# Entry of a second feed-forward on one core: where the token sums stand, and which engine shifts, scales and splits the late token tiles

## The chip, the cores and the metric

One NeuronCore of a Trainium2 chip runs the whole program. The metric is device time in microseconds of one execution; lower is better. TensorE (PE) multiplies, VectorE (DVE), ScalarE (ACT) and GpSimd (POOL) do the rest, and SyncE (SP) issues most transfers. Each engine works through its own instructions in order and waits on semaphores for the others.

## The reference

One layer of an encoder: a feed-forward, a mixer with two kinds of attention, a second feed-forward, each behind an RMS norm that is shifted and scaled. There are 512 tokens of 1024 values, in float32. What matters here is the step from the mixer's output to the second feed-forward:

```python
x = x + g2[:, None, :] * (merged @ w_out[l])
h = modulate(rmsnorm(x, ffn2_norm[l]), sh3, sc3)        # h * (1 + scale) + shift
x = x + FFN_RES_WEIGHT * g3[:, None, :] * swiglu(h, ffn2_w_in[l], ffn2_w_out[l])

def swiglu(h, w_in, w_out):
    g, u = jnp.split(h @ w_in, 2, axis=-1)               # 2 x 2816 columns
    return (jax.nn.silu(g) * u) @ w_out
```

## The kernel before

Tokens are worked on in four tiles of 128, called tile 0 to tile 3. For a precise product every matrix is split in a high part (a cast to a shorter format, on ScalarE, `split`, L202) and a low part (source minus high part, L204 on VectorE, or L208 on GpSimd), and each product is three matmuls: high by high, high by low, low by high (L223 to L225).

The mixer ends in `down`. For each token tile its last matmuls are followed on VectorE by the product with the gate (L706) and the addition to `x` (L707), on ScalarE by the sum of squares (L233), on VectorE by L240 and on GpSimd by `rstd` (L230). `norm_token` multiplies the tile by its `rstd` (L247). `turn_token`, which is held back in a list until `flush` is called, transposes the tile on TensorE (L261) in two groups of four 128x128 blocks. It shifts and scales each block on its way out of PSUM (the first of each group on VectorE, L266, three on ScalarE, L268), and splits each group into `h_hi` (ScalarE) and `h_lo` (VectorE). In the traces tiles 0 and 1 carry the name `xn` here (`xn_2_7108`, `xn_2_7141` where numbers are kept), tiles 2 and 3 `sc` (`sc4_7189`, `sc4_7243`).

The second feed-forward begins with four plain jobs in `up_plain`: job 0 and 1 are the gate and up columns of the first 128 hidden units, job 2 and 3 those of the next. A job's weights are loaded into a buffer `raw` (four of them, in turn), cast to `wh`, subtracted to `wl`. The first three jobs come in two halves: TensorE turns tile 2, does the first half of job 0 (tokens of tiles 0 and 1), the first half of job 1, turns tile 3, does the first half of job 2; then the second halves (tiles 2 and 3) of jobs 0, 1 and 2; then job 3 whole.

Behind these `up_fast` does the other hidden units with seven products in place of eight, which need sums of token blocks. `mix_tokens(0)` forms them for tiles 0 and 1, `mix_tokens(1)` for tiles 2 and 3: four additions or subtractions on VectorE (L288 to L291) and four splits (`sum_h`, `sum_l`). The fast products also need sums of weights (`w_sums`, L616 to L620, VectorE). The products read, in turn, plain tokens, then the sums `out[0]`, `out[1]`, `out[3]`, `out[2]`.

TensorE's order is the order in which the code is written. For the other engines a scheduler sets the order when the program is built.

Of the kernel before, what the change touches and what calls it, by code (L numbers as in the profile page):

```python
# [10 lines left out]
F32 = mybir.dt.float32  # L11
# [3 lines left out]
ALU = mybir.AluOpType  # L15
# [6 lines left out]
NT = S // P  # L22
# [17 lines left out]
TURN_DVE = 1  # L40
LAG_DOWN, LAG_OUT = 2, 0
EARLY_UP, FLUSH_UP = 3, (0, 2)
# [114 lines left out]
class Block:  # L157
# [85 lines left out]
    def norm_token(self, t, which, xn):  # L243
        nc = self.nc
        if which == 2 and t < 2:
            xn = self.slot([P, D], F32, "xn_2")
        nc.vector.tensor_scalar(xn, self.x[:, t], self.rstd[:, t:t + 1], None, op0=ALU.mult)  # L247
        self.pending.append(lambda: self.turn_token(t, which, xn))

    def flush(self):  # L250
# [3 lines left out]
    def turn_token(self, t, which, xn):  # L254
        nc = self.nc
        h32 = xn.rearrange("p (k c) -> p k c", k=KT)
        ts = slice(t * P, (t + 1) * P)
        for g in range(2):
            pt = self.bank("t")
            for j in range(4):  # L260
                nc.tensor.transpose(pt[:, j * P:(j + 1) * P], xn[:, (4 * g + j) * P:(4 * g + j + 1) * P], self.ident)  # L261
            for j in range(4):
                k = 4 * g + j
                sc, sh = self.scale[which][:, k:k + 1], self.shift[which][:, k:k + 1]
                if j < TURN_DVE:
                    nc.vector.tensor_scalar(h32[:, k], pt[:, j * P:(j + 1) * P], sc, sh, op0=ALU.mult, op1=ALU.add)  # L266
                else:
                    nc.scalar.activation(h32[:, k], pt[:, j * P:(j + 1) * P], AF.Identity, scale=sc, bias=sh)  # L268
            ks = slice(4 * g, 4 * g + 4)
            self.split(h32[:, ks], self.hH[:, ks, ts], self.hL[:, ks, ts])  # L270
        if which == 2:
            self.mixed.append(h32)
# [5 lines left out]
    def mix_tokens(self, j):  # L278
        ha, hb = self.mixed[2 * j:2 * j + 2]
        if not j:  # L280
            self.sum_tiles()
        a11, a12, a21, a22 = (h[:, ks] for h in (ha, hb) for ks in (slice(0, 4), slice(4, 8)))
        cs = slice(j * P, (j + 1) * P)
        self.token_sums(a11, a12, a21, a22, [[z[:, :, cs] for z in pair] for pair in self.sums])

    def token_sums(self, a11, a12, a21, a22, out):
        tt = self.nc.vector.tensor_tensor
        tt(a22, a21, a22, op=ALU.add)  # L288
        tt(a21, a21, a11, op=ALU.subtract)
        tt(a11, a22, a11, op=ALU.subtract)  # L290
        tt(a12, a12, a11, op=ALU.subtract)  # L291
        for (hi, lo), part in zip(out, (a22, a11, a21, a12)):
            self.split(part, hi, lo)

    def sum_tiles(self):
        self.sums = [[self.slot([P, KT // 2, S // 2], F32R, "sum_" + p) for p in "hl"] for _ in range(4)]
# [22 lines left out]
    def ada_columns(self, vec):  # L319
        io, nc = self.io, self.nc  # L320
        layer, kind = divmod(vec, 3)
        res = self.ring.tile([P, KT], F32, tag="adac", name="adac", bufs=2) if kind else self.shift[layer]
        for m in range(KT):
            self.ada_dot(self.ada_load(io["w_ada"][vec, m]), vec, m, res[:, m:m + 1])
            yield m == KT - 1
        if kind:
            col = (COL_FFN1, COL_MIX, COL_FFN2)[layer]
            nc.vector.scalar_tensor_tensor(
                self.scale[layer], res, 1.0, self.cols[:, col:col + KT], op0=ALU.add, op1=ALU.mult)
        yield True  # L330
# [323 lines left out]
    def act_parts(self, u):  # L654
# [14 lines left out]
        return [[z[:, j] for z in pair] for j in range(2)]  # L669

    def down(self, parts, nk, w2, layer, tail, after, lag=0, store=None, side=None):
        nc = self.nc
        nu = nk // 2
# [410 lines left out]
    def layer(self, banks):  # L1084
        nc, io = self.nc, self.io
        self.acts, self.act_pairs, self.act_seen = [], {}, []
        for f in range(F0):
            self.swiglu(f, banks[2 * f], banks[2 * f + 1])
        self.rope_angles()
        self.up_plain(io["w1a"], range(F0, F0 + F1), {0: self.mix_all})  # L1090
        gen = self.vectors((2,))
        self.up_fast(io["w1a"], range(F0 + F1, NF), WEIGHTS_A, lambda n: self.advance(gen, n > 4))
        self.x = self.fix.tile([P, NT, D], F32, tag="x16", name="x_again")
        for t in range(NT):
            nc.scalar.dma_start(self.x[:, t], io["x"][t * P:(t + 1) * P])
        late = self.vectors((4, 3, 7, 6))
        self.ada_slots = True

        def vector_steps(hf, u):
            if u > 1 if hf < 1 else u < 9:  # L1100
                for _ in range(2):
                    self.advance(late, 1)
        self.down(self.act_parts, NF, io["w2a"], 0, 3, lambda t, xn: self.norm_token(t, 1, xn), LAG_DOWN, side=vector_steps)
        self.ada_slots = False
        self.mix(lambda t, xn: self.norm_token(t, 2, xn))

        def finish(t, o32):
            z = self.slot([P, D], F32, "out")
            nc.gpsimd.tensor_tensor(z[:, :512], self.x[:, t, :512], fin[:, :512], op=ALU.mult)
            nc.vector.tensor_tensor(z[:, 512:], self.x[:, t, 512:], fin[:, 512:], op=ALU.mult)  # L1110
            nc.scalar.mul(z[:, :512], z[:, :512], self.rstd[:, t:t + 1])
            nc.sync.dma_start(io["out"][t * P:(t + 1) * P, :512], z[:, :512])
            nc.vector.tensor_scalar(z[:, 512:], z[:, 512:], self.rstd[:, t:t + 1], None, op0=ALU.mult)
            nc.scalar.dma_start(io["out"][t * P:(t + 1) * P, 512:], z[:, 512:])
        gen = self.vectors((8,))
        self.acts, self.act_pairs, self.act_seen = [], {}, []
        for t in range(NT):
            nc.scalar.dma_start(self.x_home[t], self.x[:, t])
        mixes = {EARLY_UP + j - 1: lambda j=j: self.mix_tokens(j) for j in range(2)}
        self.up_plain(io["w1b"], range(F2), mixes, EARLY_UP, FLUSH_UP)  # L1120
        self.up_fast(io["w1b"], range(F2, NF), WEIGHTS_B)
        fin = self.gate_row("final_gain")
        nc.scalar.dma_start(fin, io["final"].to_broadcast([P, D]))
        self.x = self.fix.tile([P, NT, D], F32, tag="x16", name="x_last")
        for t in range(NT):
            nc.scalar.dma_start(self.x[:, t], self.x_home[t])
        self.ada_bank = "mm"

        def side(hf, u):
            if not hf:  # L1130
                self.advance(gen, 1 if u < 9 else 99)
        self.down(self.act_parts, NF, io["w2b"], 2, 3, finish, side=side)
# [79 lines left out]
```

## Time and profile before

| | |
|---|---|
| runs (3) | median 1093.59 us, 1091.13 to 1093.73 |
| the profiled execution | 1090.79 us, of which the span of the profile is 1088.9 |
| PE busy | 1061.0 us, 97% of the span |
| DVE busy | 770.5 us, 71% |
| ACT busy | 569.2 us, 52% |
| POOL busy | 155.9 us, 14% |
| the chain that ended last | PE 88%, DVE 5%, ACT 3%, DMA 2% |

Busy shares are averages over a program of many stages. The stage of this change lies between 731 us, where the mixer's last matmuls end, and about 766 us, in the second of the fast hidden units; it has to be read by itself. A row of the timeline gives the start, the duration, the engine, the line, the operation with result and sources, and in brackets the idle time of the engine before it with what ended it. A duration holds the instruction's fixed part too, so the next instruction of an engine often starts before the row's end.

### The profile page before, as it was taken

The numbers are of one execution on the slowest core, as the hardware profiler recorded it, in microseconds if no ns is written. First come the engines' busy times: TensorE is split into PE (matmuls) and PEld (weight loads), VectorE is DVE, ScalarE is ACT, GpSimd is POOL, SyncE is SP. The second block draws the span as 40 slices with busy tenths as digits, with TensorE's granted clock in tenths as the row PEclk, the third lists the DMA queues.
The fourth block names the chain that finished last, engine by engine and source line by source line (L and its number), as shares of the span: only waits on it lengthen the run. The fifth ranks groups of instructions, "written<-read, shape, count | busy, mean of one in ns | idle before, by whom it ended". The sixth has DMA issues, their size and how long they took to land.

```text
span 1088.9 us, 16923 instructions
## 1 busy us (share of the span) xinstructions
PE 1061.0 (97%) x6496; PEld 939.4 (86%) x6496; DVE 770.5 (71%) x1277; ACT 569.2 (52%) x1066; POOL 155.9 (14%) x222
## 2 busy tenths in 40 slices
PE   4999999999999999999999999999999999999997
PEld 3789999998888898988888887888999999988885
DVE  5898898878984766666668643569887887883524
ACT  5546555564322676767667524356655655661312
POOL 1000000000000011334544477100000000000200
PEclk9999999999999999999999999999999999999999
DMA  9633454439974611122222164623333333374312
GB/s 361 256 100 106 147 159 137 132 97 350 346 259 137 235 62 39 40 78 78 80 95 78 61 206 128 245 100 109 102 98 116 116 98 98 120 252 127 103 59 78
DMA packets 43575, 152.04 MB, mean 140 GB/s; under 512 B 5219, under 2 KB 5219, under 8 KB 43494
## 3 DMA queue, kind: packets, MB, share of 16 engines
q1 hardware_dynamic: 38160, 136.20, 37.5%
q10 hardware_dynamic: 5334, 14.76, 3.8%
q8 instruction: 51, 0.84, 0.3%
q14 instruction: 30, 0.25, 0.1%
HBM read 144.65 MB, written 6.29 MB: 139 GB/s over the span
## 4 chain that ended last, share of the span: by engine, by line
PE 88%; DVE 5%; ACT 3%; DMA 2%; issue 1%; ACTq 0%; POOLq 0%; DVEq 0%
PE ps_mm L223 10%; PE ps_mm L224 10%; PE ps_mm L225 10%; PE ps_s L595 4%; PE ps_s L593 4%; PE ps_s L594 4%; PE ps_s L225 3%; PE ps_s L224 3%; PE ps_s L223 3%; PE ps_t L594 3%; PE ps_t L593 3%; PE ps_t L595 3%; PE ps_t L225 2%; PE ps_t L223 2%; PE ps_t L224 2%; PE ps_o L593 2%
## 5 line engine op out<-in xcount | busy, mean ns | idle before, releaser
L202 ACT CAST wh<-raw 128x1024 fp32r<-128x1024 f32 x148 | 155.1, 1051 | 171.4 <-PE ps_t L225 65.6
L204 DVE TENSOR_TENSOR wl<-raw,wh 128x1024 fp32r<-128x1024 f32 x116 | 142.5, 1231 | 85.7 <-ACT wh L202 85.1
L208 POOL TENSOR_TENSOR wl<-raw,wh 128x256 fp32r<-128x256 f32 x128 | 98.2, 799 | 68.9 <-ACT wh L202 61.6
L223 PE MATMUL ps_mm<-h_hi,wh 128*128 128x512 f32 (+1 forms) x264 | 101.4, 384 | 0.0
L225 PE MATMUL ps_mm<-h_hi,wl 128*128 128x512 f32 (+1 forms) x264 | 98.9, 374 | 2.0 <-DVE wl L204 2.0
L224 PE MATMUL ps_mm<-h_lo,wh 128*128 128x512 f32 (+1 forms) x264 | 98.7, 374 | 0.2 <-DVE h_lo L204 0.2
L595 PE MATMUL ps_t<-sum_h,wl 128*128 128x256 f32 x296 | 82.8, 280 | 0.6 <-DVE wl L204 0.6
L595 PE MATMUL ps_s<-sum_h,wl 128*128 128x256 f32 x296 | 82.9, 280 | 0.1
L593 PE MATMUL ps_s<-sum_h,wh 128*128 128x256 f32 x296 | 82.9, 280 | 0.0
L594 PE MATMUL ps_t<-sum_l,wh 128*128 128x256 f32 x296 | 82.7, 279 | 0.0
L593 PE MATMUL ps_t<-sum_h,wh 128*128 128x256 f32 x296 | 82.6, 279 | 0.0
L594 PE MATMUL ps_s<-sum_l,wh 128*128 128x256 f32 x296 | 82.6, 279 | 0.0
L230 POOL TENSOR_TENSOR rstd<-ss,neghalf 128x1 f32<-128x1 f32 x16 | 10.4, 648 | 473.4 <-DVE ss L240 464.9
L225 PEld LDWEIGHTS ps_mm<-h_hi,wl 128*128 128x128 f32 x264 | 49.6, 188 | 12.0 <-DVE wl L204 2.2
L595 PEld LDWEIGHTS ps_t<-sum_h,wl 128*128 128x128 f32 x296 | 55.6, 188 | 0.8 <-DVE wl L204 0.8
L224 PEld LDWEIGHTS ps_mm<-h_lo,wh 128*128 128x128 f32 x264 | 49.8, 189 | 7.2 <-DVE h_lo L204 0.4
L595 PEld LDWEIGHTS ps_s<-sum_h,wl 128*128 128x128 f32 x296 | 55.6, 188 | 0.4 <-DVE wl L204 0.3
L593 PEld LDWEIGHTS ps_s<-sum_h,wh 128*128 128x128 f32 x296 | 55.6, 188 | 0.1
L593 PEld LDWEIGHTS ps_t<-sum_h,wh 128*128 128x128 f32 x296 | 55.7, 188 | 0.0
L223 PEld LDWEIGHTS ps_mm<-h_hi,wh 128*128 128x128 f32 x264 | 49.7, 188 | 6.9
L594 PEld LDWEIGHTS ps_s<-sum_l,wh 128*128 128x128 f32 x296 | 55.6, 188 | 0.0
L594 PEld LDWEIGHTS ps_t<-sum_l,wh 128*128 128x128 f32 x296 | 55.6, 188 | 0.0
(409 smaller groups left out, 3179.4 us busy)
## 6 DMA issues: line engine op xcount, KB each, us to landing
raw<-w1a SPq DMA_DIRECT2D x32, 512.0 KB, 3.6
ada_w<-w_ada SPq DMA_DIRECT2D x32, 512.0 KB, 6.9
raw<-w1b SPq DMA_DIRECT2D x28, 512.0 KB, 3.6
raw<-w_ada SPq DMA_DIRECT2D x24, 512.0 KB, 3.7
raw<-w2a SPq DMA_DIRECT2D x22, 512.0 KB, 3.8
raw<-w2b SPq DMA_DIRECT2D x22, 512.0 KB, 3.6
w_first<-w_first SPq DMA_DIRECT2D x16, 512.0 KB, 9.6
raw<-w_gate SPq DMA_DIRECT2D x16, 512.0 KB, 3.6
```

The lines of the kernel that those rows point to most:

```text
L202: nc.scalar.copy(hi, src)
L204: nc.vector.tensor_tensor(lo, src, hi.bitcast(F32), op=ALU.subtract)
L208: nc.gpsimd.tensor_tensor(lo[:, cs], src[:, cs], hi[:, cs].bitcast(F32), op=ALU.subtract)
L223: mm(ps, lh, rh, start=start, stop=False)
L224: mm(ps, lh, rl, start=False, stop=False)
L225: mm(ps, ll, rh, start=False, stop=stop)
L230: nc.gpsimd.tensor_tensor(out, mean, self.neghalf[:, :n], op=ALU.pow)
L593: mm(ps, hi[:, cs], lh, start=start and k == 0, stop=False, skip_group_check=not start)
L594: mm(ps, hi[:, cs], ll, start=False, stop=False, skip_group_check=not start)
L595: mm(ps, lo[:, cs], lh, start=False, stop=k == 3, skip_group_check=not start)
```

## The change

The sums of tiles 0 and 1 (`mix_tokens(0)`) are no longer asked for behind the second halves of jobs 0 to 2, but behind job 3, together with those of tiles 2 and 3. For tiles 2 and 3 all eight blocks are shifted and scaled on ScalarE. For tile 3 the multiplication by `rstd` is on ScalarE. Of the sums of tiles 0 and 1, two of the four low parts are made on GpSimd, in two pieces each.

```diff
@@ norm_token
-        nc.vector.tensor_scalar(xn, self.x[:, t], self.rstd[:, t:t + 1], None, op0=ALU.mult)
+        if which == 2 and t == NT - 1:
+            nc.scalar.mul(xn, self.x[:, t], self.rstd[:, t:t + 1])
+        else:
+            nc.vector.tensor_scalar(xn, self.x[:, t], self.rstd[:, t:t + 1], None, op0=ALU.mult)
@@ turn_token
-                if j < TURN_DVE:
+                if j < (0 if which == 2 and t > 1 else TURN_DVE):
@@ mix_tokens
-        self.token_sums(a11, a12, a21, a22, [[z[:, :, cs] for z in pair] for pair in self.sums])
-
-    def token_sums(self, a11, a12, a21, a22, out):
+        self.token_sums(a11, a12, a21, a22, [[z[:, :, cs] for z in pair] for pair in self.sums], 2 if not j else 4)
+
+    def token_sums(self, a11, a12, a21, a22, out, pooled=4):
...
-        for (hi, lo), part in zip(out, (a22, a11, a21, a12)):
-            self.split(part, hi, lo)
+        for i, ((hi, lo), part) in enumerate(zip(out, (a22, a11, a21, a12))):
+            if i < pooled:
+                self.split(part, hi, lo)
+                continue
+            self.nc.scalar.copy(hi, part)
+            for ks in (slice(0, 2), slice(2, 4)):
+                self.nc.gpsimd.tensor_tensor(lo[:, ks], part[:, ks], hi[:, ks].bitcast(F32), op=ALU.subtract)
@@ layer
-        mixes = {EARLY_UP + j - 1: lambda j=j: self.mix_tokens(j) for j in range(2)}
+        mixes = {EARLY_UP: lambda: [self.mix_tokens(j) for j in range(2)]}
```

The scheduler turns this into another order on ScalarE and VectorE. Lines below L247 shift by 3 to 8 in the changed kernel (L268 becomes L271, L288 becomes L291, L706 becomes L714).

ScalarE, from the last high part of tile 1 to the cast of job 2's weights (`wh_7341`; job 1's are `wh_7310`). Before:

```order
L202 CAST h_hi_74<-xn_2_7141 128x4x128
L202 CAST wh_7310<-raw_7308 128x1024
L268 ACTIVATE sc4_7189<-ps_t_7262,shift2_86,scale2_83 128x128 x2
L233 ACTIVATE sc4_7243,ss_89<-x_back_6904 128x512
L1118 DMA x_home3_73<-x_back_6904 128x1024
L268 ACTIVATE sc4_7189<-ps_t_7262,shift2_86,scale2_83 128x128
L268 ACTIVATE sc4_7189<-ps_t_7273,shift2_86,scale2_83 128x128
L202 CAST h_hi_74<-sc4_7189 128x4x128
L268 ACTIVATE sc4_7189<-ps_t_7273,shift2_86,scale2_83 128x128 x2
L202 CAST wh_7341<-raw_7339 128x1024
```

The same stretch in the changed kernel:

```order
L202 CAST h_hi_74<-xn_2_7141 128x4x128
L271 ACTIVATE sc4_7189<-ps_t_7262,shift2_86,scale2_83 128x128 x2
L233 ACTIVATE sc4_7243,ss_89<-x_back_6904 128x512
L1126 DMA x_home3_73<-x_back_6904 128x1024
L248 ACTIVATE sc4_7243<-x_back_6904,rstd_90 128x1024
L271 ACTIVATE sc4_7189<-ps_t_7262,shift2_86,scale2_83 128x128 x2
L271 ACTIVATE sc4_7189<-ps_t_7273,shift2_86,scale2_83 128x128
L202 CAST h_hi_74<-sc4_7189 128x4x128
L271 ACTIVATE sc4_7189<-ps_t_7273,shift2_86,scale2_83 128x128 x3
L202 CAST wh_7310<-raw_7308 128x1024
L202 CAST h_hi_74<-sc4_7189 128x4x128
L202 CAST wh_7341<-raw_7339 128x1024
```

The cast of job 1's weights has moved from the second place to the tenth row, and the new multiplication (L248) stands in front of most of tile 2's instructions.

VectorE, from the product of tile 3's mixer output with the gate to the low part of job 1's weights (`wl_7311`). Before:

```order
L706 TENSOR_TENSOR sc4_7243<-ps_o_7052,ada_acc_6487 128x512
L266 TENSOR_SCALAR sc4_7189<-ps_t_7262,scale2_83,shift2_86 128x128
L204 TENSOR_TENSOR h_lo_75<-xn_2_7141,h_hi_74 128x4x128
L707 TENSOR_TENSOR x_back_6904<-x_back_6904,sc4_7243 128x512
L266 TENSOR_SCALAR sc4_7189<-ps_t_7273,scale2_83,shift2_86 128x128
L204 TENSOR_TENSOR wl_7311<-raw_7308,wh_7310 128x1024
L240 TENSOR_TENSOR ss_89<-ss_89 128x1
L288 TENSOR_TENSOR xn_2_7141<-xn_2_7141 128x512
```

In the changed kernel, on to tile 3's low parts (`sc4_7243`):

```order
L714 TENSOR_TENSOR sc4_7243<-ps_o_7052,ada_acc_6487 128x512
L715 TENSOR_TENSOR x_back_6904<-x_back_6904,sc4_7243 128x512
L204 TENSOR_TENSOR h_lo_75<-xn_2_7141,h_hi_74 128x4x128
L291 TENSOR_TENSOR xn_2_7141<-xn_2_7141 128x512
L240 TENSOR_TENSOR ss_89<-ss_89 128x1
...
L204 TENSOR_TENSOR wl_7311<-raw_7308,wh_7310 128x1024
L204 TENSOR_TENSOR h_lo_75<-sc4_7189,h_hi_74 128x4x128
L204 TENSOR_TENSOR wl_7342<-raw_7339,wh_7341 128x1024
L624 TENSOR_TENSOR w_sums_7536<-raw_7539,raw_7537 128x1024
L625 TENSOR_TENSOR raw_7539<-raw_7537,w_sums_7536 128x512
L628 TENSOR_TENSOR w_sums_7536<-raw_7539 128x512
L204 TENSOR_TENSOR h_lo_75<-sc4_7243,h_hi_74 128x4x128 x2
```

The addition to `x` and L240 stand two places earlier; job 1's low part stands behind the four sums of tiles 0 and 1 and tile 2's first low part. The three passes of the first fast unit's weight sums, which read the buffer that job 1's weights leave, stand in front of tile 3's two low parts; before, one of them (L616) stood between the two.

## Rows read from the trace of the kernel before

**Rows 1.** Busy time by stretches: entry, and the fast units behind it.

```profile
core 0: us, PE busy (x) PEld busy (x) DVE busy (x) ACT busy (x) POOL busy (x), PEclk, DMA share, GB/s
731.00:766.00 35.00, 32.79 (x256) 30.99 (x254) 33.58 (x50) 23.04 (x42) 0.93 (x1) 1.00 0.32 106
766.00:960.00 194.00, 193.17 (x1618) 190.34 (x1618) 156.33 (x194) 113.24 (x198) 0.96 (x1) 1.00 0.37 118
```

**Rows 2.** Timeline of TensorE: starts of jobs 1 to 3 and the waits.

```profile
734.73 0.39 PE L225 MATMUL ps_mm<-h_hi,wl 128*128 128x256 f32 x1
...
737.34 1.04 PE L261 MATMUL ps_t<-ident,sc 128*128 128x128 f32 x8
738.13 0.37 PE L223 MATMUL ps_mm<-h_hi,wh 128*128 128x256 f32 x1
...
740.58 0.39 PE L225 MATMUL ps_mm<-h_hi,wl 128*128 128x256 f32 x1 [1.97 <-DVE wl L204]
...
745.04 0.38 PE L224 MATMUL ps_mm<-h_lo,wh 128*128 128x256 f32 x1 [0.20 <-DVE h_lo L204]
...
751.86 0.39 PE L223 MATMUL ps_o<-h_hi,wh 128*128 128x512 f32 x1
```

**Rows 3.** Timeline of ScalarE from 730 us.

```profile
730.39 1.04 ACT L202 CAST wh<-raw 128x1024 fp32r<-128x1024 f32 x1
...
733.25 0.63 ACT L233 ACTIVATE sc<-x_back 128x512 f32<-128x512 f32 x1 [0.39 <-DVE x_back L707]
...
734.56 0.61 ACT L202 CAST h_hi<-sc 128x512 fp32r<-128x512 f32 x1
735.07 0.81 ACT L268 ACTIVATE sc<-ps_t,shift,scale 128x128 f32<-128x128 f32 x2
735.77 1.06 ACT L202 CAST wh<-raw 128x1024 fp32r<-128x1024 f32 x1
```

**Rows 4.** Timeline of VectorE from 731 us.

```profile
731.00 0.69 DVE L706 TENSOR_TENSOR sc<-ps_o,ada_acc 128x512 f32<-128x512 f32 x1 [1.16 <-PE ps_o L225]
...
733.13 0.41 DVE L266 TENSOR_SCALAR sc<-ps_t,scale,shift 128x128 f32<-128x128 f32 x1
...
734.65 0.69 DVE L288 TENSOR_TENSOR xn<-xn 128x512 f32<-128x512 f32 x1
...
736.45 0.69 DVE L289 TENSOR_TENSOR xn<-xn,xn 128x512 f32<-128x512 f32 x1
737.17 0.69 DVE L290 TENSOR_TENSOR xn<-xn,xn 128x512 f32<-128x512 f32 x1
...
742.56 1.22 DVE L616 TENSOR_TENSOR w_sums<-raw 128x1024 f32<-128x1024 f32 x1
```

**Rows 5.** The page: GpSimd's low parts (groups), and the weights' landing (DMA issues).

```profile
L208 POOL TENSOR_TENSOR wl<-raw,wh 128x256 fp32r<-128x256 f32 x128 | 98.2, 799 | 68.9 <-ACT wh L202 61.6
...
raw<-w1b SPq DMA_DIRECT2D x28, 512.0 KB, 3.6
```

**Rows 6.** Timeline of GpSimd: rstd of tiles 2 and 3.

```profile
727.50 0.55 POOL L230 TENSOR_TENSOR rstd<-ss,neghalf 128x1 f32<-128x1 f32 x1 [6.05 <-DVE ss L240]
734.82 0.93 POOL L230 TENSOR_TENSOR rstd<-ss,neghalf 128x1 f32<-128x1 f32 x1 [6.77 <-DVE ss L240]
```

**Rows 7.** Timeline of SyncE: the load into job 1's buffer.

```profile
734.70 0.33 SPq L197 DMA_DIRECT2D raw<-w1b  x1
```

**Rows 8.** Timeline of TensorE: its last matmul.

```profile
1080.85 0.40 PE L225 MATMUL ps_o<-wh,act_l 128*128 128x512 f32 x1
```

**Rows 9.** Busy time by stretches at the program's end; columns as in rows 1.

```profile
1084.00:1085.00 1.00, 0.00 (x0) 0.00 (x0) 0.49 (x1) 0.56 (x1) 0.40 (x1) 0.73 0.00 0
1085.00:1086.00 1.00, 0.00 (x0) 0.00 (x0) 0.00 (x0) 0.16 (x1) 0.00 (x0) 0.50 0.20 72
```

**Rows 10.** Timeline of TensorE at the program's start.

```profile
18.68 1.65 PE L468 MATMUL ps_mm<-h_hi,wh 128*128 128x512 f32 x3 [1.42 <-ACT h_hi L458]
...
21.40 0.63 PE L468 MATMUL ps_o<-h_hi,wh 128*128 128x512 f32 x1
...
24.19 0.40 PE L468 MATMUL ps_o<-h_lo,wh 128*128 128x512 f32 x1
```

## The prediction

> **What bounds the kernel now.** I read the busy time by stretches first. At the entry of the second feed-forward TensorE works 32.79 of 35 us and in the 194 us behind it 193.17 [rows 1]. So from there on the end moves with TensorE one to one, and all that the entry can still give back is 2.21 us. TensorE's timeline says where these lie: 1.97 us before the third instruction of job 2 (low part of its weights late) and about 0.3 us at 745.04 (token tile 3's low part late) [rows 2]. Elsewhere the first halves of jobs 0, 1 and 2 run without a break, one per 2.7 us, and job 1's follows job 0's directly at 734.4. To see why, look at ScalarE: it casts job 1's weights at 730.39, before it turns to token tile 2 [rows 3]. VectorE is busy all through, which the change is aimed at; but TensorE waits for it at two places only.
>
> **What the change moves.** TensorE's and SyncE's instructions stand in the same order before and after. Four pieces:
>
> (a) Token sums of tiles 0 and 1 are now formed behind job 3. Their eight VectorE passes of 128x512 (0.69 us, [rows 4]) keep their number; less two, see (d). Priced at nothing: the first product that reads a sum comes one product after job 3, and job 3 is about 5.5 us of matmuls, twice a first half. Worked out at the end of this part.
>
> (b) Shift and scale of tiles 2 and 3: four VectorE instructions of 0.41 us [rows 4] become four of 0.35 us on ScalarE [rows 3], so -1.6 us on VectorE, +1.4 us on ScalarE.
>
> (c) Tile 3's multiplication by rstd moves from VectorE to ScalarE. No row shows this form there; of the bounds (a 128x512 cast, 0.61, and a 128x1024 one, 1.06, [rows 3]) I take the cast, whose size it has. Its wait matters more than its length. On ScalarE it stands in front of six of tile 2's eight shift-and-scale instructions, tile 2's two casts and the casts of the weights of jobs 1 and 2. All of them now wait for tile 3's rstd.
>
> (d) Two low parts on GpSimd: four pieces of 128x256 at 0.80 us [rows 5], 3.2 us for the 1.4 us that they took on VectorE.
>
> A consequence of (b) stands in no line of the diff: ScalarE used to have a gap while VectorE made tile 2's first quarter, and the cast of job 1's weights was put there. Now it stands behind most of tile 2, 12 instructions later, the new multiplication among them. That is the step on which I rest the forecast.
>
> **The sum, on the times of the profiled execution.**
> 1. Tile 3 of the mixer's output is done and VectorE starts at 731.00, as before [rows 4]. Product, addition (0.72 from start to start when one needs the other), a low part and a first token sum follow: x is ready at 732.4, and the sum of squares' last step, queued behind these, starts at 733.7.
> 2. GpSimd's rstd took 0.55 us alone [rows 6], and 0.93 beside the VectorE pass of two operands at 734.65 [rows 4, 6]. It again has such a pass beside it: 733.9 to 734.8. (Other bound: 734.4.)
> 3. ScalarE has done its squares by 733.2 and stands still until 734.8. Then the multiplication 1.06, three shift-and-scales 1.05, cast 0.51, three more 1.05: 738.5. Job 1's cast, 1.06: done at 739.5 instead of 731.4.
> 4. Job 1's low part on VectorE, a two-operand pass of 1.22 [rows 4]: TensorE needs it for its third instruction, 1.27 behind the start: 740.8. Before, that instruction ran at 734.73 [rows 2]. **TensorE stands 6.1 us late here**, with just two matmuls in a gap that begins at 734.7.
> 5. The 23 instructions left of job 1's half take 2.61 (734.73 to 737.34): tile 3 is turned at 743.4. Turning takes 0.79, job 2 starts at 744.2. Its weights are ready by 742.5, so its 1.97 us wait is gone; 24 instructions of 0.1135 bring the second halves to 746.95. Before, they started at 743.2.
> 6. Job 1's raw weights free a buffer when their low part ends: 740.8, before 734.70 [rows 7]. The transfer that waits for it lands 3.6 us later [rows 5], 744.4. Three weight sums that wait for it now stand on VectorE in front of tile 3's low parts: 1.22 + 0.72 + 0.72 [rows 4]. The first low part ends at 747.75; TensorE wants it at 747.05: 0.7 us more.
> 7. The instruction that ran at 745.04 comes 12 later: 747.8 + 1.36 = 749.15. **+4.1 us.** Bounds from the uncertain rows (rstd 0.55 or 0.93, multiplication 0.61 or 1.06): +3.3 to +4.1. The 3.6 is a median, so I allow -0.3 and +0.6 for the landing: +3.0 to +4.7.
> 8. The clock. In this trace it fell once TensorE had nothing to do: the last matmul starts at 1080.85 [rows 8], the granted clock is 0.73 over the microsecond from 1084 and 0.50 over the next, the lower of its two levels, 1.2 GHz [rows 9]. The gap of step 4 is 4.8 us up to its two matmuls and 6.1 in all, longer than what lies between those rows; through the 1.97 us wait of before it stayed at 1.00 [rows 1, 2]. So I take the fall, and keep both ends. What it costs is seen at the start: single matmuls last 0.63 us up to 21.40 and 0.40 at 24.19, in a run of them that began at 18.68 [rows 10]; so half speed lasts 2.7 to 5.5 us. Half speed for 4 us costs 1.9 us in job 1's half, so tile 3 is turned at 745.3. From there its own chain sets the pace: some 0.7 until the first quarter is turned, eight shift-and-scales (2.8), two casts (1.1), the last low part (0.69): 750.6 against 745.04. **+5.5 us**, bounds +5.0 to +6.9 with the clock down.
>
> Is (a) covered then? Job 3 starts at 751.86 [rows 2] + 5.5 = 757.4, so the first fast product is due at 763.0 and the first with a sum at 764.3. ScalarE, from job 0's second half on (about 752), has a cast, the table load, two more casts, two silus and eight sums of 0.51, some 9.5 us: done near 761.5; VectorE needs one more 1.22. That leaves 1.6 us to spare; without that cover each late microsecond would be TensorE's. The low parts of (d) are read by the fourth product at the earliest, 2.7 us later still.
>
> On (d), the rows show rstd stretched by 0.38 beside a VectorE pass [rows 6]; stretched as much, the four pieces take 4.7 us and stay inside their cover. The Trainium skill (SBUF — State Buffer, section "SBUF: two separate sides") says more: VectorE with two SBUF inputs and GpSimd lock each other out for a whole instruction, so that VectorE would wait too; the sum would then be +7.1, the second rival below.
>
> **Rivals.**
> - *The wait as worked out, but the clock stays up* (two matmuls lie inside the gap, and the drop was seen only behind the last matmul of all). +4.1: 1097.7 us.
> - *VectorE and GpSimd block each other in the sums*: four VectorE passes wait 0.80 each [rows 5], 3.2 us, 1.6 more than is to spare: +7.1, 1100.7 us. For it: the rstd of 0.93. Against it: the pieces fall in a stretch where VectorE also waits for ScalarE. The rule of SBUF — State Buffer in the Trainium skill, above, is this case.
> - *The cheap ends together* (rstd 0.55, multiplication 0.6, landing 3.2, clock up): +3.0 or a little less, 1096.4 us.
> - *Faster*: ScalarE gets to job 1's cast in time, and the old 2.21 us go: 1091.4 us. It decides at 732.3, the latest start of that cast for a low part at 734.6. Against it: an rstd that cannot be there before 734.4 stands in front.
> - *Nothing changes*: the moved work was hidden and stays hidden, 1093.6 us. For it: VectorE's lower load; against it the same queue.
>
> **How the numbers follow.** The profiled execution took 1090.79 us, 1.9 more than its span; with +5.5 it is 1096.3. The median of the runs shown, 1093.59, lies 2.8 us above that execution, and I put the step on the median: 1099.1 us. Chances: forecast 0.42, clock up 0.32, blocking 0.06, cheap ends 0.11, faster 0.05, nothing 0.04. 0.3% is 3.3 us, about what a measurement of this kernel can tell. Slower by more: nearly all of the forecast, three quarters of the second case, the blocking, little else: 0.70. Faster by more: 2.21 us isn't, only with luck in the runs: 0.04. Within: 0.26. Range: from the second case's low end on the lowest run (1091.1 + 3.0) to the forecast's high end (1093.6 + 6.9), widened by half a microsecond at the top: 1094.0 to 1101.0; it leaves out the faster and unchanged cases and part of the cheap one, some 2 in 10.
>
> **What would show it.** In the profile after: a ScalarE idle of about 1.5 us that GpSimd's rstd ends; job 1's cast at 738.5 rather than 730.4; a TensorE idle of 4 to 6 us in job 1's first half, released by the cast or by the low part, in place of job 2's 1.97; granted clock below 1.00 between 738 and 746 if step 8 holds; a wait for tile 3's low part near 747 with the weight sums in front; job 3 at 756 to 757.5 instead of 751.86; and nothing new behind. Wrong would be: job 1's weights on time, or a TensorE wait on the token sums.

## The result, and the profile after

The changed kernel takes 1099.24 us (median of 6 runs, 1098.58 to 1099.79), the kernel before beside it 1092.98 (6 runs): ratio 1.0061, 95% interval 1.0051 to 1.0071, so 6.3 us slower. A second series of 6 runs (e5 below) gives a median of 1101.63 us, and a ratio of 1.0071 (1.0055 to 1.0088). The profiled execution of the changed kernel took 1099.33 us, with a span of 1097.5.

Busy time by stretches, columns as in [rows 1], the kernel after:

```profile
731.00:766.00 35.00, 29.25 (x204) 26.88 (x202) 26.25 (x33) 23.97 (x44) 6.08 (x5) 0.90 0.31 100
766.00:960.00 194.00, 192.97 (x1618) 190.47 (x1619) 157.03 (x197) 110.67 (x193) 0.95 (x1) 1.00 0.34 107
...
736.00:738.00 2.00, 0.00 (x0) 0.00 (x0) 1.27 (x2) 1.71 (x3) 0.25 (x1) 1.00 0.84 344
738.00:740.00 2.00, 0.00 (x0) 0.00 (x0) 0.69 (x1) 2.00 (x7) 0.00 (x0) 0.51 0.00 0
740.00:742.00 2.00, 0.80 (x2) 0.50 (x2) 0.99 (x1) 2.00 (x4) 0.00 (x0) 0.50 0.00 0
742.00:744.00 2.00, 1.71 (x8) 1.71 (x9) 1.97 (x3) 0.44 (x1) 0.00 (x0) 0.50 0.35 102
744.00:746.00 2.00, 2.00 (x16) 2.00 (x15) 0.31 (x1) 0.00 (x0) 0.00 (x0) 0.79 0.74 201
```

In the 35 us of the entry TensorE stands idle for 5.75 us, where it was 2.21; behind it it is as busy as before. VectorE, which the change relieves, is busy 26.25 us in place of 33.58: the load did fall, and the time did not. From 738 to almost 745 the clock is granted at its lower level.

What TensorE waited for from 725 to 790 us:

```profile
engine line waited for: us in total, times, longest us
PE ps_mm L223 <- ACT wh L202: 5.0, 1, 5.0
PE ps_s L603 <- DVE wl L204: 0.7, 1, 0.7
PE ps_t L603 <- DVE wl L204: 0.6, 1, 0.6
PE ps_mm L225 <- DVE wl L204: 0.5, 1, 0.5
```

The old wait of 1.97 us at job 2 [rows 2] is gone. In its place stands one of 5.0 us, on ScalarE's cast of job 1's weights, one of 0.5 on their low part, and two new ones behind job 3, on the low part of the fast units' weights. TensorE's timeline shows where:

```profile
735.72 0.28 PE L225 MATMUL ps_mm<-h_hi,wl 128*128 128x256 f32 x1
741.03 0.58 PE L223 MATMUL ps_mm<-h_hi,wh 128*128 128x256 f32 x1 [5.03 <-ACT wh L202]
...
742.29 0.58 PE L225 MATMUL ps_mm<-h_hi,wl 128*128 128x256 f32 x1 [0.46 <-DVE wl L204]
...
746.11 1.04 PE L264 MATMUL ps_t<-ident,sc 128*128 128x128 f32 x8
...
751.60 0.39 PE L224 MATMUL ps_mm<-h_lo,wh 128*128 128x256 f32 x1
...
758.42 0.39 PE L223 MATMUL ps_o<-h_hi,wh 128*128 128x512 f32 x1
...
766.35 0.38 PE L603 MATMUL ps_t<-sum_h,wl 128*128 128x256 f32 x1 [0.58 <-DVE wl L204]
...
768.69 0.38 PE L603 MATMUL ps_s<-sum_h,wl 128*128 128x256 f32 x1 [0.67 <-DVE wl L204]
...
775.73 0.28 PE L601 MATMUL ps_s<-h_hi,wh 128*128 128x256 f32 x1
```

After the gap matmuls follow each other every 0.21 us until 744.8, where 0.1135 is the pitch at full clock. On ScalarE:

```profile
736.29 1.15 ACT L248 ACTIVATE sc<-x_back,rstd 128x1024 f32<-128x1024 f32 x1 [1.73 <-POOL rstd L230]
...
739.92 1.06 ACT L202 CAST wh<-raw 128x1024 fp32r<-128x1024 f32 x1
```

And on VectorE:

```profile
732.38 0.69 DVE L714 TENSOR_TENSOR sc<-ps_o,ada_acc 128x512 f32<-128x512 f32 x1 [1.15 <-PE ps_o L225]
...
741.01 1.23 DVE L204 TENSOR_TENSOR wl<-raw,wh 128x1024 fp32r<-128x1024 f32 x1 [1.30 <-ACT wh L202]
...
749.14 0.69 DVE L204 TENSOR_TENSOR h_lo<-sc,h_hi 128x512 fp32r<-128x512 f32 x1 [0.77 <-ACT h_hi L202]
...
760.55 1.77 DVE L624 TENSOR_TENSOR w_sums<-raw 128x1024 f32<-128x1024 f32 x1
762.24 2.38 DVE L204 TENSOR_TENSOR sum_l<-sc,sum_h 128x512 fp32r<-128x512 f32 x2
764.54 1.76 DVE L204 TENSOR_TENSOR wl<-w_sums,wh 128x1024 fp32r<-128x1024 f32 x1
```

GpSimd's rows of this stretch, tile 3's rstd and the four pieces of (d):

```profile
735.27 0.98 POOL L230 TENSOR_TENSOR rstd<-ss,neghalf 128x1 f32<-128x1 f32 x1 [5.85 <-DVE ss L240]
760.13 5.09 POOL L301 TENSOR_TENSOR sum_l<-xn,sum_h 128x256 fp32r<-128x256 f32 x4 [23.87 <-ACT sum_h L299]
```

ScalarE stands still until tile 3's rstd comes, and casts job 1's weights at 739.92 instead of 730.39 [rows 3].

To compare executions I count from the start of VectorE's product for tile 3's mixer output (L706, here L714), called the origin from here on: 731.00 before [rows 4], 732.38 here. This takes out the 1.38 us by which this execution came later to the entry. Job 3 starts at 20.86 before [rows 2] and at 758.42 - 732.38 = 26.04 here, 5.2 later. The two waits behind job 3 add 1.25; the first product of the second fast unit starts at 36.72 before and 43.35 here (775.73 above), 6.6 later. Its row before:

```profile
767.72 0.28 PE L593 MATMUL ps_s<-h_hi,wh 128*128 128x256 f32 x1
```

With the 1.4 us ahead of the origin and 0.5 in the rest of the program, that is the 8.5 us between the two profiled executions. The profiled execution of before was a quick one, 2.2 us below the median beside it, so the medians stand only 6.3 apart.

### The profile page after: what moved, and what is told of

Its sections match the earlier page's. It is cut to its first block, busy times and chain, and to the rows that moved or that the text cites. A ratio compares the mean times of both kernels' runs of the same rounds, so it can differ in the third digit from the quotient of the medians.

```text
span 1097.5 us, 16928 instructions
## 1 busy us (share of the span) xinstructions
PE 1065.1 (97%) x6496; PEld 942.8 (86%) x6496; DVE 771.1 (70%) x1270; ACT 572.4 (52%) x1071; POOL 161.2 (15%) x226
## 4 chain that ended last, share of the span: by engine, by line
PE 87%; DVE 6%; ACT 3%; DMA 2%; issue 1%; ACTq 0%; POOL 0%; POOLq 0%; DVEq 0%
PE ps_mm L223 10%; PE ps_mm L224 10%; PE ps_mm L225 10%; PE ps_s L603 5%; PE ps_s L601 5%; PE ps_s L602 4%; PE ps_s L225 3%; PE ps_s L224 3%; PE ps_s L223 3%; PE ps_t L602 3%; PE ps_t L601 3%; PE ps_t L603 3%; PE ps_t L225 2%; PE ps_t L223 2%; PE ps_t L224 2%; PE ps_o L601 2%
```

## The experiments

All are timed beside the kernel before (ratio with its 95% interval; 0.001 is 1.1 us). None leaves out part of the computation.

**e1: shift and scale back on VectorE** (piece (b) undone).

```diff
-                if j < (0 if which == 2 and t > 1 else TURN_DVE):
+                if j < TURN_DVE:
```

> The changed kernel with piece (b) undone: VectorE again shifts and scales the first block of each group of tiles 2 and 3; (a), (c) and (d) stay. The built order puts the cast of job 1's weights back in front of tile 2, although the multiplication by rstd stays on ScalarE. Theory (the price hangs on the place of that cast): no wait in job 1's half, no fall of the clock, job 2's old wait of about 2 us stays, and up to 1.5 us of the sums' waits at the first fast unit stay: before +0.3 to +2 us, ratio 1.000 to 1.002. Rival (the price is ScalarE standing still for rstd in front of tile 2): the stall stays, ratio 1.004 to 1.006.

Measured: 1.0012 (1.0001 to 1.0023), within the theory's range. The scheduler puts the cast of job 1's weights back in its old place, right behind tile 1's last high part, although the new multiplication is still on ScalarE. The 5.0 us wait shrinks to 0.3; others take its place: 0.9 where tile 3 is turned (banks that ScalarE still reads for tile 2), 1.2 on a low part of weights, and the same 0.6 and 0.7 behind job 3. (Against the theory the clock falls in this profile too, and job 3 starts at 24.1; that execution took 1.9 us more than the median of e1, so the profile shows more of a loss than the runs have.) Piece (b), whose instructions weigh 1.6 us less on one engine and 1.4 more on the other, carries most of the loss through the order that follows from it.

**e2: the multiplication by rstd back on VectorE** (piece (c) undone).

```diff
-        if which == 2 and t == NT - 1:
-            nc.scalar.mul(xn, self.x[:, t], self.rstd[:, t:t + 1])
-        else:
-            nc.vector.tensor_scalar(xn, self.x[:, t], self.rstd[:, t:t + 1], None, op0=ALU.mult)
+        nc.vector.tensor_scalar(xn, self.x[:, t], self.rstd[:, t:t + 1], None, op0=ALU.mult)
```

> The changed kernel with piece (c) undone: tile 3's multiplication by rstd is back on VectorE; (a), (b) and (d) stay, and job 1's cast stays behind tile 2. Theory: ScalarE no longer stands still for rstd, so job 1's cast ends some 2.8 us earlier than in the changed kernel; TensorE's gap shrinks from 6.1 to about 3.3 us, the clock perhaps stays up, job 2's wait is gone: before +2 to +3.5 us, ratio 1.002 to 1.003. Rival (the late place of the cast costs little by itself, the wait for rstd is all): ratio 1.000 to 1.001.

Measured: 1.0043 (1.0029 to 1.0057). ScalarE no longer stands still for rstd and the wait for the cast falls from 5.0 to 2.2 us, but one of 1.5 for the low part follows it, the clock falls to 0.50 all the same, and job 3 starts at 25.4: with 1.8 us less of waiting at the entry it comes 0.6 earlier. The theory, which hoped for a clock that stays up, had 1.002 to 1.003.

**e3: the two low parts back on VectorE** (piece (d) undone).

```diff
-        self.token_sums(a11, a12, a21, a22, [[z[:, :, cs] for z in pair] for pair in self.sums], 2 if not j else 4)
+        self.token_sums(a11, a12, a21, a22, [[z[:, :, cs] for z in pair] for pair in self.sums], 4)
```

> The changed kernel with piece (d) undone: all low parts of the token sums on VectorE again. In the profile after, VectorE's passes of 764.54 and before are stretched beside GpSimd's four pieces, and TensorE waits twice for low parts of weights at the first fast unit (0.6 and 0.7 us). Theory (VectorE and GpSimd hold each other up there): both waits shrink or go, 1.0 to 1.6 us less than the changed kernel, ratio 1.0045 to 1.005; the stall and the fall of the clock in job 1 are as they were. Rival (VectorE is late there anyway, since two passes more come back to it): within 0.4 us of the changed kernel, ratio 1.006.

Measured: 1.0040 (1.0028 to 1.0053). The waits at the entry are the same, 5.0 and 0.5 us; both waits behind job 3 are gone. GpSimd's help was not covered, as the theory said (it had 1.0045 to 1.005).

**e4: 32 matmuls in the gap.** `FILL` is 32; the lines that define it and `nc` are left out here. Nobody reads their result; ScalarE's and VectorE's order stays that of the changed kernel.

```diff
                 mms(job, 0, S // 2)
+                if i == 0:
+                    spare = self.bank("s")
+                    hi = units[job][0]
+                    for r in range(FILL):
+                        nc.tensor.matmul(spare[:, :256], hi[:, :P], self.hH[:, 0, :256], start=True, stop=True)
```

> The changed kernel with 32 extra matmuls of 256 columns on TensorE between job 0's and job 1's first halves, into a PSUM bank that nobody reads; 3.6 us of work inside the gap of 6 us, the order of all other engines the same. Theory (the fall of the clock has a price of its own): granted clock stays at 1.00, job 1's half takes 2.6 us instead of 3.8, and the kernel gets 1.0 to 1.5 us faster than the changed one for doing more: ratio 1.0045 to 1.005. Rival (the half speed is hidden behind tile 3's own chain and the transfer): the clock stays up and the time is the changed kernel's, ratio 1.006.

Measured: 1.0047 (1.0034 to 1.0059). The ratio is the theory's, but not for its reason: the run does not isolate the clock. With 1.3 and 0.8 us of waits left the granted clock fell anyway, only later (0.69 from 740 to 742, 0.50 from 742 to 744). Job 3 starts at 26.4.

**e5: the changed kernel once more**, beside the next three.

> The changed kernel once more, beside the three that follow. Every theory: about 1.006 of the kernel before, TensorE waits about 5.0 us for the cast of job 1's weights, the granted clock falls to 0.50 and job 3 starts about 26 us behind VectorE's product for tile 3.

Measured: 1.0071 (1.0055 to 1.0088), and job 3 at 27.48, 1.4 later than in the first profile with the same waits. The difference is the clock (this execution, 1104.30 us, was the slowest of its six). Stretches of e5, in which TensorE stands still from 738.2 to 743.2:

```profile
742.00:744.00 2.00, 0.72 (x2) 0.42 (x2) 0.77 (x1) 2.00 (x4) 0.00 (x0) 0.84 0.00 0
744.00:746.00 2.00, 1.49 (x7) 1.50 (x8) 2.00 (x3) 0.66 (x1) 0.00 (x0) 0.50 0.21 49
746.00:748.00 2.00, 2.00 (x11) 2.00 (x11) 0.19 (x1) 0.00 (x0) 0.00 (x0) 0.50 0.85 266
```

Here the clock falls at about 743.4 (a mean of 0.84 over 2 us is 0.64 us at half), when the gap is over, and all but half a microsecond of the time at half speed, to about 750.2, is time in which TensorE has work (11 matmuls in 2 us; e7 below has 20). In the first profile it fell 2 us into the gap, and half of the slow time was spent waiting anyway.

**e6: the weights' casts ahead of the tokens' work**, all four pieces of the change kept. Casts and low parts are still put in order by the scheduler, but the code now asks for the weights of jobs 0 to 2 before job 0's first half.

```diff
-            units[job] = self.unit(D, w1[f, gu])
+            for ahead in jobs[:max(early, i + 1)]:
+                if ahead not in units:
+                    units[ahead] = self.unit(D, w1[ahead])
```

> The changed kernel with one thing put back: ScalarE casts the weights of jobs 1 and 2 before it turns to token tile 2, so they no longer stand behind tile 3's rstd; sums, shift and scale, multiplication and the two low parts stay where the change put them. Theory (the price is the place of that cast in ScalarE's queue): the 5.0 us wait goes and job 2's old 1.97 us too; the next thing late is tile 3's low part, worked out at 11.7 us behind VectorE's product for tile 3 and needed at 10.5, so some 1.2 us; clock at 1.00; job 3 starts at 19.5 to 20.9 (26.0 with the change, 20.9 before); the wait of about 1.3 us on the low parts of the sums' weights stays. Total 0 to -1 us from before plus that: ratio to before 0.999 to 1.001. Rival (the load moved to ScalarE and the sums behind job 3 cost by themselves, wherever the cast stands): 2 to 4 us remain, ratio 1.002 to 1.004.

Measured: 1.0021 (1.0011 to 1.0031), so 4 to 5.5 us of the loss go with the place of the cast. Not all, against what the theory expected; job 3 starts at 22.7 and not by 20.9. e8 below shows that most of the rest is (d). TensorE's waits in e6:

```profile
PE ps_t L264 <- ACT sc L271: 2.7, 2, 1.5
PE ps_s L605 <- DVE wl L204: 0.7, 1, 0.7
PE ps_t L605 <- DVE wl L204: 0.6, 1, 0.6
```

ScalarE in e6 shows why:

```profile
735.90 1.16 ACT L248 ACTIVATE sc<-x_back,rstd 128x1024 f32<-128x1024 f32 x1 [2.09 <-POOL rstd L230]
736.96 1.03 ACT L202 CAST wh<-raw 128x1024 fp32r<-128x1024 f32 x1
737.90 1.84 ACT L271 ACTIVATE sc<-ps_t,shift,scale 128x128 f32<-128x128 f32 x5
```

It still stands 2.09 us in front of the multiplication, and now all of tile 2's shift and scale comes behind it; TensorE cannot turn tile 3 into banks that still hold tile 2. The clock falls here too, to 0.50 between 742 and 744.

**e7: 52 matmuls in the gap**, the edit of e4 with FILL = 52.

> The changed kernel with 52 more 128x256 matmuls behind job 0's first half, 5.9 us of them, whose result nobody reads: they fill the whole of TensorE's gap, so job 1's third instruction runs at the same time as without them and only the clock differs. Theory (the late weights cost some 4 us and the clock 1.4 more): the clock stays at 1.00 through job 1, job 3 starts at 24.5 to 25.0 us behind VectorE's product for tile 3 (26.0 without the fill), total 1.0 to 1.5 us below the changed kernel. Rival (the clock's fall costs nothing, since tile 3's own chain sets the pace): job 3 at 26.0, total as the changed kernel's. If the clock falls in spite of a full TensorE: nothing told.

Measured: 1.0037 (1.0024 to 1.0050). Stretches of e7:

```profile
738.00:740.00 2.00, 2.00 (x20) 2.00 (x19) 0.69 (x1) 2.00 (x5) 0.00 (x0) 1.00 0.04 8
740.00:742.00 2.00, 1.79 (x16) 1.59 (x15) 1.63 (x2) 1.80 (x3) 0.00 (x0) 1.00 0.00 0
742.00:744.00 2.00, 2.00 (x20) 2.00 (x19) 1.33 (x2) 0.00 (x0) 0.00 (x0) 1.00 0.69 172
```

The clock stays at 1.00, and the weights are as late as ever: job 1's third instruction runs at 9.94 behind the origin, 9.91 in the changed kernel. Job 3 starts at 25.25 instead of 26.04 (e5: 27.48). So the late weights by themselves cost 4.4 us at job 3, and the clock 0.8 to 2.2 on top, by when it falls. That is read from single profiles. By the ratios e7 lies 2.6 and 3.7 us below the two series of the changed kernel, so the clock's part is shown, and its size only roughly.

**e8: e6 with (d) undone as well.**

> As the one before last, and the two low parts on VectorE again in place of GpSimd. Theory (GpSimd's pieces and VectorE's passes stretch each other, which makes the low parts of the sums' weights about 1.3 us late): that wait goes, so the total is about 1.3 us below the kernel with the early casts alone: ratio to before 0.998 to 0.999. Rival (the sums are late since they stand behind job 3, whoever makes the low parts): the wait stays or grows by the 1.4 us that VectorE gets back, ratio 0.999 to 1.002.

Measured: 1.0004 (0.9996 to 1.0013). Both waits behind job 3 go, as the theory said; the 2.7 us at tile 3's turning stay, and the total stays above the theory's 0.999. e3 and e8 differ by the edit of e6 alone and are both free of (d): 1.0040 to 1.0004. (The profiles of e6 and e8 can't be compared at job 3: with the same waits there the clock is at half for 3.4 us in e6 and for 6.8 us in e8, and job 3 starts at 22.7 and 24.0.)

**e9: the sums behind job 3, and nothing else** (piece (a) alone, low parts all on VectorE). Against the kernel before:

```diff
-        mixes = {EARLY_UP + j - 1: lambda j=j: self.mix_tokens(j) for j in range(2)}
+        mixes = {EARLY_UP: lambda: [self.mix_tokens(j) for j in range(2)]}
```

> The kernel before with piece (a) alone: the sums of both pairs of tiles behind job 3, their low parts all on VectorE; shift and scale, multiplication by rstd as before. The prediction priced this at nothing: job 2's wait of about 2 us stays (its low part stands on VectorE behind the first shift and scale of tile 3, not behind the sums), job 3 starts 20 to 21 us behind VectorE's product for tile 3, no wait on the sums; ratio to before 0.999 to 1.001. Rival (sums behind job 3 come too late by themselves): a wait of 1 us or more at the products of the second fast unit, ratio 1.001 to 1.002.

Measured: 1.0003 (0.9993 to 1.0013), one wait of 1.95 us at job 2, none at the sums: nothing, as priced.

**e10: the sums behind job 3 and two of their low parts on GpSimd** ((a) and (d)).

> The kernel before with pieces (a) and (d): as the one ahead, and two low parts on GpSimd. Theory (GpSimd's pieces and VectorE's passes stretch each other wherever they meet): the two waits on the low parts of the sums' weights are there as with the whole change, 0.6 and 0.7 us, and nothing else is new: 1.3 us above the one ahead, ratio to before 1.000 to 1.002. Rival (they are late only because the whole entry is): no such wait, ratio 0.999 to 1.001.

Measured: 1.0013 (1.0002 to 1.0024). TensorE's waits in e10:

```profile
PE ps_mm L225 <- DVE wl L204: 1.9, 1, 1.9
PE ps_s L600 <- DVE wl L204: 0.7, 1, 0.7
PE ps_t L600 <- DVE wl L204: 0.3, 1, 0.3
```

GpSimd and VectorE in e10:

```profile
754.60 5.08 POOL L298 TENSOR_TENSOR sum_l<-xn,sum_h 128x256 fp32r<-128x256 f32 x4 [17.49 <-ACT sum_h L296]
...
755.02 1.76 DVE L621 TENSOR_TENSOR w_sums<-raw 128x1024 f32<-128x1024 f32 x1
```

The waits are there although the entry is on time, and so is the stretching: (d) costs by itself. (The two ratios alone would not show it; their intervals overlap.)

These two also show something that neither was made for. The same wait of 1.95 us at job 2 stands in both. Stretches of e9:

```profile
740.00:742.00 2.00, 1.69 (x10) 1.69 (x11) 2.00 (x5) 1.72 (x5) 0.00 (x0) 0.75 0.39 70
742.00:744.00 2.00, 2.00 (x12) 2.00 (x11) 1.97 (x3) 0.99 (x3) 0.00 (x0) 0.50 0.50 195
```

And of e10:

```profile
740.00:742.00 2.00, 0.07 (x1) 0.07 (x1) 2.00 (x4) 1.19 (x4) 0.00 (x0) 1.00 0.00 0
742.00:744.00 2.00, 2.00 (x17) 2.00 (x18) 2.00 (x4) 1.75 (x4) 0.00 (x0) 1.00 0.54 109
```

In e9 the clock falls behind it and job 3 starts at 21.97; in e10, as in the profile of before, it stays up, and job 3 starts at 20.75.

**e11 and e12: towards a better kernel.** e11 is the kernel before with the edit of e6; e12 has the sums behind job 3 as well.

> The kernel before with the casts of job 1's and job 2's weights ahead of tile 2 on ScalarE and VectorE. Theory (a weights' cast ahead of the tokens' work is what the entry wants): job 2's wait of 1.97 us goes, tile 3's low part is then late by up to 1 us, job 3 starts at 19 to 20.5 us behind VectorE's product for tile 3; ratio to before 0.998 to 0.9995. Rival (tile 2's shift and scale, put later by it, keeps the banks that tile 3 is turned into, as it did in the changed kernel with early casts): 2 to 3 us of waits at tile 3's turning, the clock falls, ratio 1.001 to 1.003.

> The one ahead with the sums of both pairs behind job 3 as well, so that VectorE has nothing but the entry's own work in front of it. Theory: no wait above 1 us is left at the entry, job 3 at 19 to 20 us, ratio 0.998 to 0.999. Rival: as for the one ahead, 1.001 to 1.003.

Measured: 1.0013 (1.0001 to 1.0025) and 1.0016 (1.0007 to 1.0025). Job 2's wait is gone in both, and the tokens are late instead, with the clock down to 0.50 behind it. The wait of e12 (e11 has 2.3 and 0.3 at the same place):

```profile
PE ps_mm L223 <- ACT h_hi L202: 2.9, 1, 2.9
```

Neither theory's place was right: it is tile 3's high part at the second halves, not its turning. ScalarE is not busy in front of it but stands still, in e12 for 3.67 us (2.56 in e11), until VectorE has shifted and scaled tile 3's first block:

```profile
740.59 1.50 ACT L268 ACTIVATE sc<-ps_t,shift,scale 128x128 f32<-128x128 f32 x4 [3.67 <-DVE sc L266]
...
737.80 1.22 DVE L623 TENSOR_TENSOR w_sums<-raw 128x1024 f32<-128x1024 f32 x1 [0.83 <-DMA raw<-w1b]
...
740.15 0.72 DVE L266 TENSOR_SCALAR sc<-ps_t,scale,shift 128x128 f32<-128x128 f32 x2
```

On VectorE the first pass of the fast unit's weight sums now stands in front of tile 2's low parts and tile 3's shift and scale, and it waits 0.83 us for its load. In the kernel before it stood behind them, at 742.56 [rows 4]. So the edit that brings the cast forward has moved an instruction on the other engine too, and that one is in the way.

## Why the prediction was right, and where it was off

**Time.** 1099.1 was predicted, 1099.24 measured; the step put on the median was +5.5, the medians differ by 6.3. That the two times agree to 0.1 us is luck: the kernel before was 0.6 us quicker beside it than in the runs that the sum started from, and the step 0.8 us larger; the second series of the same kernel has its median at 1101.63, above the range's 1101.0. The late cast, the wait that it causes and the fall of the clock stood as forecast. Two terms were off: (d), whose effect on VectorE the forecast put at nothing, and the size of the clock's part. Of the signs, "nothing new behind" failed: the two waits of 1.25 us stand there, on weights though and not on token sums.

**Steps 1 to 4, the late cast: right.** With 1.38 us taken off each time of the profile after, for its later origin: rstd starts at 733.89 (733.9 predicted), takes 0.98 (0.93); ScalarE's idle of 1.73 is ended by it (1.5 or so); the multiplication takes 1.15 (1.06); job 1's cast ends at 739.60 (739.5); its third instruction runs at 740.91 (740.8). That the place of this cast is the price is shown by e6: put back, it takes 4 to 5.5 us off with all four pieces kept, and the pair e3 and e8 gives 3.9. What brings it there is shown by e1: undoing (b) alone returns it. That ScalarE's standstill lengthens it is shown by e2.

**Steps 5 to 7: right.** Without the clock +4.1 was predicted at job 3; e7, with the clock up, shows 4.4. Step 6's wait behind the weight sums is there too, 0.33 us of it where 0.7 was predicted: in e7 VectorE goes from them straight to tile 3's first low part (its high part had been ready since 747.28), and TensorE's instruction runs at 16.78 behind the origin (the low part was predicted to end at 16.75).

```profile
747.75 0.68 DVE L205 TENSOR_TENSOR h_lo<-sc,h_hi 128x512 fp32r<-128x512 f32 x1
...
748.49 0.39 PE L225 MATMUL ps_mm<-h_lo,wh 128*128 128x256 f32 x1 [0.33 <-DVE h_lo L205]
```

With the clock down it does not come: in the profile after, VectorE is done with the weight sums and then waits 0.77 us more for tile 3's high part. There tile 3's own chain set the pace, as step 8 had it.

**Step 8, the clock: the fall right, its size a matter of the execution.** Half speed was taken to last 4 us of matmuls, to cost job 1's half 1.9 us and the whole 1.4. In the first profile it costs job 1's half 1.2 us (3.82 from its third instruction to tile 3's turning, where 2.61 was the time before); tile 3 is turned at 744.7 (745.3), its low part is used at 750.2 (750.6), and the price at job 3 is 0.8. In e5 it is 2.2. The reason given for the fall does not hold as put: the clock staying at 1.00 through a 1.97 us wait was read as telling short gaps from long ones, and e9 shows it falling behind a gap of that very length. The rival "the clock stays up", given 0.32, was right in its sum only, which e7 bears out.

**"Is (a) covered": right for (a), wrong for (d).** (a) alone costs nothing (e9). ScalarE is done with its sums and casts at 761.2 (761.5 predicted, again less 1.38), and the 1.6 us to spare were there: unstretched, VectorE's passes from 760.55 on would have ended by 764.1, and TensorE came for the low part at 765.6 (both on the times of the profile after as they stand). What ate them is (d). Beside GpSimd's pieces VectorE's passes took 1.77 and 1.76 where one takes 1.22 [rows 4], and 2.38 for two where two take 1.29: 2.2 us in all. GpSimd's four pieces took 5.09, where four at the mean of the pieces before take 3.2 [rows 5] and 4.7 was allowed. So it is the second rival, blocking, given 0.06, that happened: its +7.1 is the forecast's +5.5 with 1.6 us of waits added, and the profiles show +5.2 at job 3, 1.25 us of waits behind it and +6.6 at the second fast unit. It was oversized a little: VectorE lost 2.2 us and not four times 0.80. The step that failed is "stretched as much, the four pieces take 4.7 us and stay inside their cover": it stretched GpSimd alone and left VectorE as it was. The Trainium skill (SBUF — State Buffer, section "SBUF: two separate sides") says that a VectorE pass with two SBUF inputs and a GpSimd instruction that reads SBUF lock each other out; the rows of the profile after and of e10 agree that both lose time, VectorE some 0.5 us per pass of 128x1024. Three pairs price (d): the changed kernel and e3, 1.0061 to 1.0040; e6 and e8, 1.0021 to 1.0004; e10 and e9, 1.0013 to 1.0003. That is 1.1 to 2.3 us; each ratio is known to about 0.001, so the pairs show that (d) costs something near the 1.25 us of waits and not more exactly.

**The rival "faster" was priced wrongly.** It held that a cast in time gives back the old 2.21 us. e6, e11 and e12 have the cast in time, and none is faster than before: other waits of 2.3 to 2.9 us come in place of job 2's, and the clock falls. They are not one cause. In e6 ScalarE works from 735.90 until tile 3's last high part without a pause, so there its own time between tile 3's rstd and TensorE's need is short. In e11 and e12 ScalarE waits for VectorE, where the weight sums have come in front of tile 3. A kernel with the early cast and the weight sums kept behind tile 3 was not run, so what an early cast could give back is open.

**Open.** The sum of the parts (4.4, 0.8 to 2.2, 1.25) is 6.5 to 7.9 us at the entry; the medians show 6.3 and 8.4 in the two series. How often the clock falls behind job 2's wait in the kernel before, unprofiled, is not known; each fall would lift its time by about 1.2 us (e9 against e10), and its runs spread over 3.2 to 4.5 us in a series. Why two executions of the changed kernel reach the origin 2.2 us apart (732.38 and, in e5, 734.59; 729.67 to 734.59 over all the kernels) was not looked into. The fill of e7 was not tried on a kernel without (d).

## What to carry to other kernels

Relieving the busiest engine is worth what the wait that it ends is worth, and its price is the place that the moved work takes in the other engine's queue: list what stands behind it there, above all the casts that TensorE needs next, and what the moved work itself waits for. Putting one instruction back early can move others (e11, e12), so read the new order of every engine. A pass moved to GpSimd beside a stretch of two-operand passes on VectorE is paid on both engines; count both. And a gap on TensorE can cost, on top of its length, a time at half clock that differs from one execution to the next, so shortening a gap may give back less than what was cut from it (e2: 1.8 us less of waits, job 3 0.6 earlier).

## What the runs showed of the hardware that was not expected

- The granted clock fell 2 us into a gap of 5.0 us in one profile of the changed kernel and at the end of the same gap in another (e5): the program is the same, and job 3 is 1.4 us apart. It stayed at half for some 6.8 us in both, and in e1, e2, e3, e8 and e12; in e4, e6, e9 and e11 for some 3.4 us.
- It fell behind a single gap of 1.95 us in e9 and not behind the same gap in e10 or the 1.97 us of before.
- It fell in e1, e2 and e4 in or behind two or three short gaps near each other (0.9, 0.3 and 1.2 us; 2.2 and 1.5; 1.3 and 0.8), and stayed up in e7, where TensorE had two waits of 0.2 and 0.3 us.
- VectorE's passes of 128x1024 took 1.76 to 1.78 us beside GpSimd's subtractions in the profiles after, e5, e7 and e10, and about 1.22 without them.
